# Decoder trunk in fp32: order of the products in the seven-product quads, one more such quad per layer, another split of the buffers

## The chip, the cores and the metric

One NeuronCore of a Trainium2 chip runs the whole program; the other cores have no work. The metric is the device time of one execution in microseconds. Engines named below: TensorE (PE in the profile, matmul and transpose), VectorE (DVE), ScalarE (ACT), GpSimd (POOL; here it mostly issues transfers) and SyncE (SP; its queue issues the weight loads).

## The reference

Two post-norm layers over 256 tokens of width 2048. Each layer mixes tokens with two attention groups (a sparse one with a top-k indexer, and a latent one, whose low-rank latents `cq` and `ckv` go through an RMS norm) and then runs a SwiGLU feed-forward of width 5632.

```python
proj = einsum('bsd,de->bse', x, w_in)
out_a = sparse_attention(...)                      # qa, ka, va, indexer qi, ki, wi
q_b  = rms_norm(cq, g_cq) @ w_uq;  kv = rms_norm(ckv, g_ckv) @ w_ukv
x = layer_norm(ALPHA * x + concat(out_a, out_b) @ w_o)
h = silu(x @ w_gate) * (x @ w_up)                  # w_gate, w_up: 2048 x 5632
x = layer_norm(ALPHA * x + h @ w_down)
```

## The kernel before

**Tiles and splits.** Tokens stand in two tiles of 128. Weights arrive in units of 128 x 1024 fp32 (two contraction slices of 128 x 512 columns, 512 KB). A unit is loaded by SP into a `raw` buffer; ScalarE rounds it into `wh` (line 324) and VectorE makes the rest `wl = raw - wh` (line 325). A `wh` and a `wl` are a pair. A product of two slices is six matmuls of 512 columns: `wh` with the high and with the low part of the tokens, `wl` with the high part, for each slice (lines 346 to 348, and 932 to 935 in the feed-forward).

**The feed-forward.** The 5632 columns go in 11 blocks of 512. Block 0 is done plainly (`gu`, 8 units for gate, 8 for up). Blocks 1 to 10 run `gate_up`: four quads, each over a unit `u`, its partner `u + 4`, gate and up. A plain quad (N) multiplies 2 tokens tiles x 2 units x 2 matrices, 8 products. A seven-product quad (S, `wino_quad`) is the Strassen-Winograd form: 7 products, from four matrix blocks `r11`, `r21` (gate), `r22` (up) and `r12`, the last the sum of two up units that a second, accumulating transfer on GpSimd's queue makes in a `sum` buffer; three more sums are made by VectorE in place in the raw buffers. Its token operands `s1` to `s4` are made once per layer (`sum_operands`). Block 1 was N N N S, block 2 is N S N S, blocks 3 to 10 are S S N S. In the last quad of a block VectorE also combines the product banks into gate and up: the lines with `on(...)`, line 970 in the profile, tiles `e` and `g`. Banks 2 and 3 hold `p6` and `p7`; `c11`, `c21` lie in banks 4 and 5, `c12` and `c22` in the pair named `att`.

**The order.** From block 3 on, `down_half` runs ahead of each `gate_up`: two columns of the down projection of earlier blocks, 8 units, 96 matmuls; its first column uses banks 2 and 3. A scheduler that works from priorities lays each engine's instructions into one fixed order when the kernel is built; at run time each engine follows its order and waits where an operand or a buffer is not ready. Work beside the matmuls (`spawn`, `tick`) is spread in steps: `yield n` lets `n` units of matmul work pass. `hidden` (lines 898 to 903) ends a block: silu, a product `g = g * e`, a transpose. `affine` (lines 431 to 434) is a layer norm's gain and bias, in blocks 0 to 2, from broadcast loads `g` and `b`.

**Buffers in the phase called more** (the last pass of the output projection, the feed-forward, and the first input block of the next layer): raw buffers 4 and 1 more, pairs 5 and 3 more, two sum buffers. A raw buffer is taken again after as many loads as there are buffers. The first pass of such a phase multiplies all 8 units of a matrix with the first token tile while the second tile is still being normalised, then the same 8 units with the second.

**The latents.** `tb_post` (line 587) normalises both latents and transposes them: for each of the two token tiles, transposes on TensorE into the two `tr` banks, then copies and differences by ScalarE and VectorE (`ckvT`, `cqT`, `kpT`).

Of the kernel before, what the change touches and what calls it, by code (L numbers as in the profile page):

```python
# [53 lines left out]
NKT = D // P  # L54
NFC = FFN // C
RAW = 4
UNITS, MORE = 5, 3
RAWMORE, RAWSUM = 1, 2
HALF = NKT // KU // 2
SOONER = 60  # L60
SOON = 200
# [19 lines left out]
def hybrid_trunk(ctx: ExitStack, tc: tile.TileContext, x, xt_in, pos, w_in, g_cq, g_ckv, w_uq,  # L81
                 w_ukv, w_o, ln1_g, ln1_b, ln1_T, w_gu, w_down, ln2_g, ln2_b, ln2_T, out):
    nc = tc.nc
# [6 lines left out]
    def nm(s):  # L90
        uid[0] += 1
        return f"{s}{uid[0]}"
# [23 lines left out]
    def t2(shape, s, dt=F32):  # L116
        if phase["name"] == "att":
            phase["t2"] = phase.get("t2", 0) + 1
            if phase["t2"] * T2MORE % (T2 + T2MORE) < T2MORE:
                return pt(shape, dt, s, "t2", T2MORE)  # L120
        return sb.tile(shape, dt, name=nm(s), tag="t2", bufs=T2)
# [17 lines left out]
    def trp():  # L139
        return in_turn("tr", 4, 2)  # L140
# [125 lines left out]
    def step(task):  # L266
        try:
            task[0] = units_gone[0] + (next(task[1]) or 1)
        except StopIteration:
            tasks.remove(task)  # L270

    def tick():
        units_gone[0] += 1
        for task in list(tasks):
            if task in tasks and task[0] <= units_gone[0]:
                step(task)
# [242 lines left out]
    def layer(l, xh, xl, norms, last):  # L519
# [76 lines left out]
        def tb_post(o):  # L596
            gq = t2([P, QL], "gq")
            gk = t2([P, KVL], "gk")
            nc.gpsimd.dma_start(gq, g_cq[l].partition_broadcast(P))
            nc.gpsimd.dma_start(gk, g_ckv[l].partition_broadcast(P))  # L600
            ckv = t2([P, NT, KVL], "ckv")
            sd = []
            for t in range(NT):
                nc.scalar.activation(cq[t][:, 432:512], o[t][:, 0:80], AF.Copy)
                nc.scalar.activation(ckv[:, t, :], o[t][:, 80:336], AF.Copy)
                sd.append(dup_rope(o[t][:, 336:400], cosM[:, t], sinM[:, t], M_ROPE))
            ys = [(rms(ckv[:, t, :], KVL, gk), rms(cq[t], QL, gq)) for t in range(NT)]
            yield 3
            for t, (yk, yq) in enumerate(ys):
                yield 1  # L610
                tp, tq = trp(), trp()
                rms_T(yk, KVL, tp[:, P:])
                dup_T(sd[t], tp)
                rms_T(yq, QL, tq)
                rms_out(KVL, ckvT, t, tp[:, P:])
                dup_out(kpT, t, tp)
                rms_out(QL, cqT, t, tq)
# [136 lines left out]
        if l == 0:  # L754
            turn("att")
            o = in_chunk(QI0, load_xT)
# [3 lines left out]
        else:  # L760
            o = in_chunk(QI0, None, lambda: finish(*norms))
# [10 lines left out]
        o = in_chunk(TA)  # L772
        p_ta = spawn(ta_post(o))
        o = in_chunk(QI1)
        p_qi1 = spawn(heads_T(o, 8, I_DIM, I_ROT, cosI, sinI, qiT[1]))
        p_ix = spawn(indexer())
        o = in_chunk(TB)
# [5 lines left out]
        o = proj([(w_uq[2][l, u], range(u * KU, (u + 1) * KU)) for u in range(QL // P // KU)], cqk, C)  # L783
# [26 lines left out]
        for c in range(D // C):  # L810
            o = proj([(w_o[l, c, k // KU], range(k, k + KU)) for k in first], olhs, C)
# [79 lines left out]
        def slhs(name):  # L891
            return lambda k: sums[name, k]
# [23 lines left out]
        def gate_up(fc, order, between):  # L916


            o, begun = {}, set()

            def passes(name, lhs, ks, w, final):
                if name not in o:
                    if name in BANKS:
                        o[name] = bank(BANKS[name], "gu_" + name)
                    else:
                        pair = o["up"] = att()
                        o["c12"], o["c22"] = pair[:, 0, :], pair[:, 1, :]
                for j, k in enumerate(ks):
                    h, l = lhs(k)
                    a, b = w[0][:, j, :], w[1][:, j, :]  # L930
                    end = final and j == len(ks) - 1
                    mm(o[name], h, a, start=name not in begun, stop=False)  # L932
                    begun.add(name)
                    mm(o[name], h, b, start=False, stop=False)  # L934
                    mm(o[name], l, a, start=False, stop=end)  # L935

            def token(t):
                return lambda k: xk(t, k)

            def unit(u):  # L940
                return range(u * KU, (u + 1) * KU)

            def plain_quad(u, first, lastz):
                for i, col in enumerate(("c11 c21", "c12 c22")):
                    vs = (u, u + HALF)
                    ws = [load_unit(w_gu[i][l, fc, v], KU * C) for v in vs] if first else [None, None]
                    for a in range(2):
                        for b in range(2):


                            t, j = (a, b) if first else (b, a)
                            if ws[j] is None:
                                ws[j] = load_unit(w_gu[i][l, fc, vs[j]], KU * C)
                            name = col.split()[t]
                            passes(name, token(t), unit(vs[j]), ws[j], lastz and i == 1 and a == b == 1)
                        tick()

            def wino_quad(u, final):
                ADD, SUB = ALU.add, ALU.subtract
                r12 = load_sum(w_gu[1][l, fc, u], w_gu[1][l, fc, u + HALF])  # L960
                r11, r21, r22 = (load_raw(w_gu[i][l, fc, v], KU * C) for i, v in ((0, u), (0, u + HALF), (1, u + HALF)))

                def p(i, lhs, raw, ks):
                    w = parts(raw, KU * C)
                    name = INTO.get(i, i)
                    passes(name, lhs, ks, w, final)

                def on(d, x, y, op):
                    with tc.high_priority(offset=SOONER):
                        nc.vector.tensor_tensor(d, x, y, op=op)  # L970

                if final:
                    e = phase["pool"].tile([P, NT, C], F32, name=nm("e"), tag="e", bufs=1)
                    g = phase["pool"].tile([P, NT, C], F32, name=nm("g"), tag="silu", bufs=1)
                lo_, hi_ = unit(u), unit(u + HALF)
                p("p1", token(0), r11, lo_)
                if final:
                    with tc.high_priority(offset=SOONER):
                        nc.scalar.activation(e[:, 0, :], o["p1"], AF.Copy)
                p("p2", token(0), r21, hi_)  # L980
                if final:
                    on(g[:, 0, :], e[:, 0, :], o["c11"], ADD)
                tick()
                nc.vector.tensor_tensor(r11, r12, r11, op=ADD)
                p("p6", slhs("s2"), r11, lo_)
                if final:
                    on(e[:, 0, :], o["p6"], e[:, 0, :], SUB)
                nc.vector.tensor_tensor(r21, r11, r21, op=ADD)
                p("p7", slhs("s3"), r12, lo_)
                if final:  # L990
                    on(e[:, 1, :], e[:, 0, :], o["p7"], ADD)
                tick()
                p("p4", token(1), r21, hi_)
                if final:
                    on(g[:, 1, :], o["c21"], e[:, 1, :], SUB)
                nc.vector.tensor_tensor(r11, r11, r22, op=SUB)
                p("p5", slhs("s1"), r11, lo_)
                if final:
                    on(e, e, o["p5"].unsqueeze(1).to_broadcast([P, NT, C]), ADD)
                tick()  # L1000
                p("p3", slhs("s4"), r22, lo_)
                if final:
                    on(e, e, o["up"], ADD)
                tick()
                if final:
                    return g, e

            lastp = max(i for i, q in enumerate(order) if q[0] == "plain")
            for i, (kind, u) in enumerate(order):
                if kind == "plain":  # L1010
                    plain_quad(u, i == 0, i == lastp)
                else:
                    r = wino_quad(u, i == len(order) - 1)
                if i == 0 and between:
                    between()
            return r
# [40 lines left out]
        def finish_hidden():  # L1057
            finish(*[h[2] for h in held])

        ORDER = {1: "NNNS", 2: "NSNS"}  # L1060
        UNIT = {"NNNS": (0, 1, 2, 3), "NSNS": (0, 2, 1, 3), "SSNS": (1, 2, 0, 3)}

        g = gu(0, 0, lambda: finish(*norms))
        affine(ln1_g[l], ln1_b[l], 0, ALPHA)
# [4 lines left out]
        for fc in range(1, NFC):  # L1069
            order = ORDER.get(fc, "SSNS")  # L1070
            if fc >= FIRSTD:
                down_half(fc)
                finish_hidden()
            g, u = gate_up(fc, [({"N": "plain", "S": "wino"}[k], v) for k, v in zip(order, UNIT[order])],
                           finish_hidden if fc < FIRSTD else None)
# [72 lines left out]
```

## Time and profile before

| what | value |
|---|---|
| three runs | 2189.41, 2189.73 and 2197.02 us, median 2189.73 |
| the profiled execution | 2196.58 us, of which the span from first to last instruction is 2194.5 us |
| mean granted TensorE clock | 0.997 |
| TensorE, matmul | busy 2157.3 us |
| VectorE | busy 1741.2 us |
| ScalarE | busy 1238.0 us |
| transfers | 204 GB/s read and written over the span |

The busy time of an engine is the union of its instructions' durations; matmuls overlap, so the start-to-start distance, not the printed duration, is what one costs. The profiled execution is one of the slower kind: it stands 6.9 us above the median of the runs.

### The profile page before, as it was taken

What the parts mean: (1) busy time and instruction counts of PE and PEld (TensorE: products, weight loads), DVE (VectorE), ACT (ScalarE), POOL (GpSimd) and SP (SyncE); (2) the same over time, 40 slices, a digit from 0 to 9 for tenths busy, and PEclk for the clock granted to TensorE, in tenths of its full rate; (3) what the DMA queues carried; (4) which work ended last, traced back from release to release, by engine and by line L of the source; (5) the groups of instructions that cost most, each with busy time, mean ns of one, the idle gap of its engine ahead of it and who ended that gap; (6) DMA issues with size and microseconds to landing.
All of it is one profiled execution on the core that took longest, in us unless ns stands there. A gap on an engine that the chain in (4) does not pass through costs nothing.

```text
span 2194.5 us, 28019 instructions
## 1 busy us (share of the span) xinstructions
PE 2157.3 (98%) x10044; PEld 1790.1 (82%) x10044; DVE 1741.2 (79%) x2227; ACT 1238.0 (56%) x1619; POOL 156.0 (7%) x254
## 2 busy tenths in 40 slices
PE   8999999999999999999999999999999999999997
PEld 7888888888888878888888888888887888877886
DVE  6685557889898889888657757678897889989885
ACT  5555454656565666656545554446565566656653
POOL 0100000001001011000101000000010001101101
PEclk9999999999999999999999999999999999999999
DMA  8544457557887787787745455666677788788785
GB/s 299 166 164 150 154 180 251 190 175 242 242 259 222 235 257 238 237 247 233 232 140 169 158 171 181 205 226 205 197 226 226 234 253 245 224 252 231 236 288 145
DMA packets 136364, 471.14 MB, mean 215 GB/s; under 512 B 15409, under 2 KB 15713, under 8 KB 135585
## 3 DMA queue, kind: packets, MB, share of 16 engines
q1 hardware_dynamic: 113760, 409.13, 54.8%
q0 software_dynamic: 22320, 60.09, 14.2%
q8 instruction: 79, 1.29, 0.2%
q14 instruction: 61, 0.49, 0.1%
q10 hardware_dynamic: 144, 0.13, 0.0%
HBM read 445.69 MB, written 2.10 MB: 204 GB/s over the span
## 4 chain that ended last, share of the span: by engine, by line
PE 66%; DVE 12%; issue 9%; DMA 9%; ACT 2%; POOL 1%; POOLq 0%; ACTq 0%; DVEq 0%; SPq 0%
PE acc L346 14%; PE acc L348 14%; PE acc L347 14%; DVE wl L325 7%; DMA raw<-in_w_gate_dram 4%; DMA raw<-in_w_down_dram 3%; PE tr L366 2%; ACT wh L324 2%; PE gu_p L932 2%; PE gu_p L935 2%; PE gu_p L934 2%; PE gu_c L932 2%; PE gu_c L935 2%; PE gu_c L934 2%; PE att L932 1%
## 5 line engine op out<-in xcount | busy, mean ns | idle before, releaser
L324 ACT ACTIVATE wh<-raw 128x1024 fp32r<-128x1024 f32 (+1 forms) x864 | 896.4, 1054 | 750.8 <-PE acc L348 208.1
L325 DVE TENSOR_TENSOR wl<-raw,wh 128x1024 fp32r<-128x1024 f32 (+1 forms) x864 | 1035.0, 1218 | 352.4 <-ACT wh L324 347.8
L346 PE MATMUL acc<-wh,xh 128*128 128x512 f32 (+1 forms) x768 | 304.1, 396 | 6.0 <-ACT wh L324 6.0
L348 PE MATMUL acc<-wh,xl 128*128 128x512 f32 (+1 forms) x768 | 298.6, 389 | 0.0
L347 PE MATMUL acc<-wl,xh 128*128 128x512 f32 (+1 forms) x768 | 297.6, 388 | 0.0
L346 PE MATMUL acc<-wh,hT 128*128 128x512 f32 x640 | 251.4, 393 | 13.7 <-DVE e L970 13.5
L347 PE MATMUL acc<-wl,hT 128*128 128x512 f32 x640 | 249.9, 390 | 0.0
L348 PE MATMUL acc<-wh,hT 128*128 128x512 f32 x640 | 249.8, 390 | 0.0
L346 PEld LDWEIGHTS acc<-wh,xh 128*128 128x128 f32 x768 | 145.2, 189 | 36.5 <-ACT wh L324 6.0
L348 PEld LDWEIGHTS acc<-wh,xl 128*128 128x128 f32 x768 | 144.9, 189 | 28.9 <-DVE xl L412 0.8
L347 PEld LDWEIGHTS acc<-wl,xh 128*128 128x128 f32 x768 | 145.3, 189 | 26.6 <-DVE wl L325 0.7
L932 PE MATMUL gu_c<-wh,xh 128*128 128x512 f32 x424 | 165.1, 389 | 0.0
L935 PE MATMUL gu_c<-wh,xl 128*128 128x512 f32 x424 | 165.0, 389 | 0.0
L934 PE MATMUL gu_c<-wl,xh 128*128 128x512 f32 x424 | 164.9, 389 | 0.0
L346 PEld LDWEIGHTS acc<-wh,hT 128*128 128x128 f32 x640 | 120.5, 188 | 44.0 <-DVE e L970 18.5
L348 PEld LDWEIGHTS acc<-wh,hT 128*128 128x128 f32 x640 | 120.6, 188 | 25.3
L347 PEld LDWEIGHTS acc<-wl,hT 128*128 128x128 f32 x640 | 120.5, 188 | 24.6
L313 POOL DMA_DIRECT2D sum<-in_w_up_dram x54 | 46.2, 856 | 906.5 <-DVE wl L325 396.3
L1035 POOL DMA_DIRECT2D x<-d x80 | 74.3, 1070 | 495.5 <-ACT d L1034 490.9
L935 PEld LDWEIGHTS gu_c<-wh,xl 128*128 128x128 f32 x424 | 79.6, 188 | 16.7
L934 PEld LDWEIGHTS gu_c<-wl,xh 128*128 128x128 f32 x424 | 79.6, 188 | 16.6
L932 PEld LDWEIGHTS gu_c<-wh,xh 128*128 128x128 f32 x424 | 79.6, 188 | 16.5
(287 smaller groups left out, 3552.8 us busy)
## 6 DMA issues: line engine op xcount, KB each, us to landing
raw<-in_w_gate_dram SPq DMA_DIRECT2D x176, 512.0 KB, 5.2
raw<-in_w_down_dram SPq DMA_DIRECT2D x176, 512.0 KB, 6.1
raw<-in_w_in_dram SPq DMA_DIRECT2D x144, 512.0 KB, 3.6
raw<-in_w_up_dram SPq DMA_DIRECT2D x122, 512.0 KB, 4.6
raw<-in_w_o_dram SPq DMA_DIRECT2D x64, 512.0 KB, 4.3
sum<-in_w_up_dram SPq DMA_DIRECT2D x54, 512.0 KB, 3.3
sum<-in_w_up_dram POOLq DMA_DIRECT2D x54, 512.0 KB, 8.4
x<-d POOLq DMA_DIRECT2D x80, 256.0 KB, 7.9
```

What stands on the lines that cost most here:

```text
L313: nc.gpsimd.dma_start(raw, b, accum_op=ALU.add)
L324: nc.scalar.activation(wh[:, :n], raw[:, :n], AF.Copy)
L325: nc.vector.tensor_tensor(wl[:, :n], raw[:, :n], f(wh[:, :n]), op=ALU.subtract)
L346: mm(o[t][:, :n], h, a, start=first, stop=False)
L347: mm(o[t][:, :n], h, b, start=False, stop=False)
L348: mm(o[t][:, :n], l, a, start=False, stop=final)
L366: nc.tensor.transpose(psum[:, i * P:(i + 1) * P], s, ident)
L932: mm(o[name], h, a, start=name not in begun, stop=False)
L934: mm(o[name], h, b, start=False, stop=False)
L935: mm(o[name], l, a, start=False, stop=end)
L1035: nc.gpsimd.dma_start(xt[t][:, c * C:(c + 1) * C], d, accum_op=ALU.add)
```

## The change

Five things, in the diff below. (1) In a seven-product quad the product `p3` is made third, ahead of the sums, and the last sum is written over the block `r22` that `p3` has read instead of over `r11`; the bank pair of up is added into `e` ahead of `p5`. The order of the products is now p1 p2 p3 p6 p7 p4 p5; it was p1 p2 p6 p7 p4 p5 p3. (2) Pairs in the phase called more go from eight to seven. (3) Raw buffers go from five to seven. (4) Block 1 becomes N S N S, so each layer has one seven-product quad more. (5) The latents of the first token tile are transposed one unit of matmul work earlier; those of the second stay where they were.

```diff
--- before.py
+++ after.py
@@ -54,8 +54,8 @@
 NKT = D // P
 NFC = FFN // C
 RAW = 4
-UNITS, MORE = 5, 3
-RAWMORE, RAWSUM = 1, 2
+UNITS, MORE = 5, 2
+RAWMORE, RAWSUM = 3, 2
 HALF = NKT // KU // 2
 SOONER = 60
 SOON = 200
@@ -607,7 +607,8 @@
             ys = [(rms(ckv[:, t, :], KVL, gk), rms(cq[t], QL, gq)) for t in range(NT)]
             yield 3
             for t, (yk, yq) in enumerate(ys):
-                yield 1
+                if t:
+                    yield 2
                 tp, tq = trp(), trp()
                 rms_T(yk, KVL, tp[:, P:])
                 dup_T(sd[t], tp)
@@ -981,26 +982,25 @@
                 if final:
                     on(g[:, 0, :], e[:, 0, :], o["c11"], ADD)
                 tick()
+                p("p3", slhs("s4"), r22, lo_)
                 nc.vector.tensor_tensor(r11, r12, r11, op=ADD)
                 p("p6", slhs("s2"), r11, lo_)
                 if final:
                     on(e[:, 0, :], o["p6"], e[:, 0, :], SUB)
+                tick()
                 nc.vector.tensor_tensor(r21, r11, r21, op=ADD)
                 p("p7", slhs("s3"), r12, lo_)
                 if final:
                     on(e[:, 1, :], e[:, 0, :], o["p7"], ADD)
-                tick()
+                nc.vector.tensor_tensor(r22, r11, r22, op=SUB)
                 p("p4", token(1), r21, hi_)
                 if final:
                     on(g[:, 1, :], o["c21"], e[:, 1, :], SUB)
-                nc.vector.tensor_tensor(r11, r11, r22, op=SUB)
-                p("p5", slhs("s1"), r11, lo_)
+                    on(e, e, o["up"], ADD)
+                tick()
+                p("p5", slhs("s1"), r22, lo_)
                 if final:
                     on(e, e, o["p5"].unsqueeze(1).to_broadcast([P, NT, C]), ADD)
-                tick()
-                p("p3", slhs("s4"), r22, lo_)
-                if final:
-                    on(e, e, o["up"], ADD)
                 tick()
                 if final:
                     return g, e
@@ -1057,8 +1057,8 @@
         def finish_hidden():
             finish(*[h[2] for h in held])
 
-        ORDER = {1: "NNNS", 2: "NSNS"}
-        UNIT = {"NNNS": (0, 1, 2, 3), "NSNS": (0, 2, 1, 3), "SSNS": (1, 2, 0, 3)}
+        ORDER = {1: "NSNS", 2: "NSNS"}
+        UNIT = {"NSNS": (0, 2, 1, 3), "SSNS": (1, 2, 0, 3)}
 
         g = gu(0, 0, lambda: finish(*norms))
         affine(ln1_g[l], ln1_b[l], 0, ALPHA)
```

What moves, engine by engine. First SP's loads around the last quad of a block (block 4 of layer 0; the `in_w_gate` and `in_w_up` loads at the top are that quad's own, the `in_w_down` loads belong to the down half that follows it). Before:

```order
L306 DMA raw_5666<-in_w_gate_dram 128x1024
L306 DMA raw_5668<-in_w_gate_dram 128x1024
L306 DMA raw_5670<-in_w_up_dram 128x1024
L306 DMA raw_5760<-in_w_down_dram 128x1024
L306 DMA raw_5778<-in_w_down_dram 128x1024
L312 DMA sum_6021<-in_w_up_dram 128x1024
L306 DMA raw_5796<-in_w_down_dram 128x1024
L306 DMA raw_5814<-in_w_down_dram 128x1024
L306 DMA raw_5840<-in_w_down_dram 128x1024
```

Now:

```order
L306 DMA raw_5676<-in_w_gate_dram 128x1024
L306 DMA raw_5678<-in_w_gate_dram 128x1024
L306 DMA raw_5680<-in_w_up_dram 128x1024
L306 DMA raw_5770<-in_w_down_dram 128x1024
L306 DMA raw_5788<-in_w_down_dram 128x1024
L306 DMA raw_5806<-in_w_down_dram 128x1024
L306 DMA raw_5824<-in_w_down_dram 128x1024
L306 DMA raw_5850<-in_w_down_dram 128x1024
L312 DMA sum_6031<-in_w_up_dram 128x1024
L306 DMA raw_5868<-in_w_down_dram 128x1024
```

The sum for a later quad stood ahead of the third down load and now stands ahead of the sixth. What the order does not show: the third down load takes the buffer of the last quad's `r11` before, of a plain unit loaded ahead of that quad now.

Next ScalarE around the latents in layer 0 (`rel` are the indexer's scores; `tr_1131` and `tr_1132` before, `tr_1113` and `tr_1114` now, are the first token tile's two banks, `tr_1176` the second's). Before:

```order
L636 ACTIVATE rel_1105<-att_1100 128x512
L636 ACTIVATE rel_1107<-att_1100 128x512
L324 ACTIVATE wh_1272<-raw_1270 128x1024
L369 ACTIVATE ckvT_396<-tr_1131 128x2x128
L369 ACTIVATE cqT_395<-tr_1132 128x4x128
L563 ACTIVATE kpT_390<-tr_1131 128x128
L324 ACTIVATE wh_1293<-raw_1291 128x1024
L636 ACTIVATE rel_1168<-att_1163 128x512
```

Now:

```order
L637 ACTIVATE rel_1105<-att_1100 128x512
L369 ACTIVATE ckvT_396<-tr_1113 128x2x128
L637 ACTIVATE rel_1107<-att_1100 128x512
L369 ACTIVATE cqT_395<-tr_1114 128x4x128
L563 ACTIVATE kpT_390<-tr_1113 128x128
L324 ACTIVATE wh_1272<-raw_1270 128x1024
L324 ACTIVATE wh_1293<-raw_1291 128x1024
L637 ACTIVATE rel_1168<-att_1163 128x512
```

The three readings of the first tile's banks moved ahead of two weight roundings and into the scores; the second tile's reading keeps its row. VectorE's difference for `ckvT` stood behind seven small rows of the top-k and a weight difference, and now stands among the scores.

Last, VectorE in block 1 of layer 0, from the end of the gain and bias on (`x_64`, `x_65` are the token tiles; `hT` belongs to block 0). Before:

```order
L325 TENSOR_TENSOR wl_4222<-raw_4219,wh_4221 128x1024
L370 TENSOR_TENSOR hT_4034<-tr_4103,hT_4034 128x4x128
L370 TENSOR_TENSOR hT_4034<-tr_4110,hT_4034 128x4x128
L433 TENSOR_TENSOR x_64<-x_64,g_4368 128x512
L433 TENSOR_TENSOR x_65<-x_65,g_4368 128x512
L325 TENSOR_TENSOR wl_4240<-raw_4237,wh_4239 128x1024
L325 TENSOR_TENSOR wl_4258<-raw_4255,wh_4257 128x1024
L434 TENSOR_TENSOR x_64<-x_64,b_4369 128x512
L434 TENSOR_TENSOR x_65<-x_65,b_4369 128x512
L325 TENSOR_TENSOR wl_4285<-raw_4276,wh_4284 128x1024
```

Now:

```order
L325 TENSOR_TENSOR wl_4171<-raw_4132,wh_4170 128x1024
L991 TENSOR_TENSOR raw_4134<-raw_4132,raw_4134 128x1024
L325 TENSOR_TENSOR wl_4183<-sum_4129,wh_4182 128x1024
L370 TENSOR_TENSOR hT_4034<-tr_4103,hT_4034 128x4x128
L370 TENSOR_TENSOR hT_4034<-tr_4110,hT_4034 128x4x128
L995 TENSOR_TENSOR raw_4136<-raw_4132,raw_4136 128x1024
L325 TENSOR_TENSOR wl_4195<-raw_4134,wh_4194 128x1024
L433 TENSOR_TENSOR x_64<-x_64,g_4378 128x512
L325 TENSOR_TENSOR wl_4205<-raw_4136,wh_4204 128x1024
L325 TENSOR_TENSOR wl_4218<-raw_4215,wh_4217 128x1024
L325 TENSOR_TENSOR wl_4236<-raw_4233,wh_4235 128x1024
L325 TENSOR_TENSOR wl_4254<-raw_4251,wh_4253 128x1024
```

Where plain units followed, the seven-product quad's parts and sums now stand. From the end of the last row on `b_4025`, just ahead of these, up to and with the row `g = g * e` that ends block 1, VectorE had 37 rows, 23 of 1024 columns and 14 of 512; it has 44 now, 30 and 14. The transposes that read this `g` stand 36 matmuls into block 2, before and now. Layer 1 has the same rows.

One more place, in words: in the first pass the eighth unit's pair can only be made when the first unit's pair is done with, so TensorE's order now has the first unit's six matmuls with the second token tile ahead of the eighth unit. From the end of those six to the first use of the eighth `wh` stand five matmuls and a transpose group, to the first use of its `wl` four matmuls more.

## Rows read from the trace of the kernel before

**Rows 1.** The page, part 1: busy time, share of span, instructions

```profile
PE 2157.3 (98%) x10044; PEld 1790.1 (82%) x10044; DVE 1741.2 (79%) x2227; ACT 1238.0 (56%) x1619; POOL 156.0 (7%) x254
```

**Rows 2.** TensorE's waits: who ended them, total us, times, longest

```profile
PE acc L346 <- DVE e L970: 13.5, 9, 4.3
...
PE tr L366 <- ACT kpT L563: 3.5, 2, 1.9
PE att L932 <- DVE e L970: 1.3, 1, 1.3
```

**Rows 3.** Timeline, TensorE, 1667 to 1675 us: start, duration, idle before

```profile
1667.39 0.39 PE L935 MATMUL att<-wh,many 128*128 128x512 f32 x1
...
1669.43 0.39 PE L348 MATMUL acc<-wh,hT 128*128 128x512 f32 x1
1674.12 0.65 PE L346 MATMUL acc<-wh,hT 128*128 128x512 f32 x1 [4.30 <-DVE e L970]
```

**Rows 4.** Timeline, 1661 to 1674 us: VectorE, ScalarE, DMA issues, landing

```profile
1666.81 0.69 DVE L970 TENSOR_TENSOR e<-gu_p,e 128x512 f32<-128x512 f32 x1
1672.24 1.22 DVE L325 TENSOR_TENSOR wl<-raw,wh 128x1024 fp32r<-128x1024 f32 x1 [4.75 <-ACT wh L324]
1673.39 0.68 DVE L970 TENSOR_TENSOR e<-e,gu_p 128x512 f32<-128x512 f32 x1
...
1671.16 1.06 ACT L324 ACTIVATE wh<-raw 128x1024 fp32r<-128x1024 f32 x1 [6.20 <-DMA raw<-in_w_down_dram]
...
1661.62 12.20 SPq L306 DMA_DIRECT2D raw<-in_w_down_dram  x6
...
raw<-in_w_down_dram SPq DMA_DIRECT2D x176, 512.0 KB, 6.1
```

**Rows 5.** Windows: length, busy time of each engine, granted clock, DMA

```profile
117.20:121.20 4.00, 3.29 (x12) 2.91 (x13) 3.31 (x8) 3.23 (x7) 0.00 (x0) 0.58 0.43 140
1674.10:1678.00 3.90, 3.88 (x10) 3.06 (x11) 3.90 (x5) 3.89 (x5) 0.00 (x0) 0.56 0.77 234
776.00:780.00 4.00, 3.07 (x13) 2.55 (x14) 3.69 (x5) 2.59 (x3) 0.00 (x0) 1.00 1.03 406
```

**Rows 6.** Timeline, 102 to 118 us: TensorE, ScalarE, VectorE

```profile
107.36 1.13 PE L631 MATMUL att<-kiT,qiT 64*128 64x256 f32 x8
...
111.28 0.38 PE L366 MATMUL tr<-ident,rn 128*128 128x128 f32 x2
...
117.91 0.69 PE L366 MATMUL tr<-ident,rn 128*128 128x128 f32 x2 [1.88 <-ACT kpT L563]
...
117.58 0.28 ACT L563 ACTIVATE kpT<-tr 128x128 f32<-128x128 f32 x1 [4.28 <-DVE ckvT L370]
...
102.95 0.75 DVE L585 SCALAR_TENSOR_TENSOR rn<-cq,rrs,gq 128x512 f32<-128x512 f32 x1 [0.34 <-POOL rrs L584]
...
117.13 0.42 DVE L370 TENSOR_TENSOR ckvT<-tr,ckvT 128x256 fp32r<-128x256 f32 x1
```

**Rows 7.** Windows over feed-forward blocks 3 to 10, layer 0: their sum

```profile
sum 504.40, PE 499.48 PEld 412.16 DVE 448.40 ACT 306.49 POOL 46.30; mean PE 62.43 PEld 51.52 DVE 56.05 ACT 38.31 POOL 5.79
```

**Rows 8.** Timeline, blocks 1 and 2 of layer 0: VectorE, then TensorE

```profile
443.81 1.29 DVE L433 TENSOR_TENSOR x<-x,g 128x512 f32<-128x512 f32 x2 [1.90 <-ACT g L431]
445.48 1.29 DVE L434 TENSOR_TENSOR x<-x,b 128x512 f32<-128x512 f32 x2 [0.37 <-ACT b L431]
...
466.88 4.63 DVE L325 TENSOR_TENSOR wl<-raw,wh 128x1024 fp32r<-128x1024 f32 x4
...
486.15 1.22 DVE L903 TENSOR_TENSOR g<-g,e 128x1024 f32<-128x1024 f32 x1
...
488.07 1.03 PE L366 MATMUL tr<-ident,g 128*128 128x128 f32 x8
```

**Rows 9.** A weight pair's ScalarE copy; ScalarE at the first pass

```profile
L324 ACT ACTIVATE wh<-raw 128x1024 fp32r<-128x1024 f32 (+1 forms) x864 | 896.4, 1054 | 750.8 <-PE acc L348 208.1
...
401.01 1.50 ACT L409 ACTIVATE v<-att,gbT 128x128 f32<-128x128 f32 x4 [0.33 <-ACT v L409]
```

## The prediction

> **What bounds the kernel now.** The page first: TensorE is busy for 98% of the span [rows 1], so time is won by fewer matmuls or fewer waits of TensorE. The timeline [rows 3] gives the price of a matmul of 512 columns: 9 starts in 2.04 us, 0.227 us each. It also shows that a wait costs 0.16 us more than the idle time printed, since 4.69 us lie between the two starts where 0.227 would, 4.46 too many, and 4.30 are printed. The waits by releaser come next [rows 2]: 13.5 us in nine waits of the down projection's first matmul on VectorE's `e` rows, 3.5 us in two waits of the latents' transposes on ScalarE's `kpT`, 1.3 us at the start of block 2's `att`. The timeline behind the longest tells the mechanism [rows 4]. VectorE finished `e` from p6 at 1667.5 and came to `e` from p7, which empties the bank that down wants, only at 1673.4. It stood 4.75 us before a `wl` row, for a `wh` that ScalarE could not make until a down load landed. Issue of the six down loads behind the sum began at 1661.6, when the last quad gave buffers back, and a down load takes 6.1 us to land in the median. So the cause is five raw buffers, three of them held by the last quad. VectorE is not short of time: in blocks 3 to 10 it is busy 56.05 us against 62.43 us of TensorE [rows 7]. Last the clock [rows 5]: behind this wait it was granted 0.56 for 3.9 us, behind the first latent wait 0.58 for 4.0 us (the lower level, 1.2 instead of 2.4 GHz, for most of that time), so each cost 0.44 x 3.9 or 0.42 x 4.0, 1.7 us more.
>
> **(a) Fewer matmuls.** A seven-product quad has one product of two slices, 6 matmuls, less. Two layers: 12 x 0.227 = **-2.7 us**.
>
> **(b) Latents.** The second tile's transposes at 117.91 waited for the first tile's `kpT`, which waited 4.28 us for VectorE's `ckvT` difference at 117.13, although the first tile had been transposed at 111.28 [rows 6]. Now these transposes stand right behind the score matmuls that begin at 107.36, 12 matmuls (2.7 us) earlier, and the copies and differences move ahead of weight work and top-k rows. Their data is there: the first tile's last latent row on VectorE began at 102.95 and took 0.75. The wait was shorter than the move, and VectorE's rows in front of the difference go too, so I take both waits and the one clock loss as gone: 3.5 + 2 x 0.16 + 1.7 = **-5.5 us**; the other bound is 0.
>
> **(c) Raw buffers, seven for five.** Three down parts still stand ahead of `e` from p7, but the first four down loads now take the buffers of plain units, free long before, and the sum no longer stands in front of the third. The fifth takes that of `r11`, released when the last sum is written; VectorE then has seven rows of 1024 columns and four of 512 to do before that load's part, 10 us by the prices under (d), against 6.1. So the nine waits should go: 13.5 + 9 x 0.16 + 1.7 for the clock = 16.6 us. I take nine tenths, **-15 us**, since loads that land late can leave some; the bounds are 0 and -16.6. Seven pairs instead of eight cost nothing there: VectorE's 6.4 us of slack per block hide the shorter lead. Without that cover it is up to one product, 1.36 us, for each of the 16 blocks.
>
> Against this stands a rule. The Trainium skill (Trainium Kernel Development and Optimization, Key Constraints) says that transfers of all queues run on the same 16 DMA engines and interleave. By it more loads in flight would only land later each, and (c) would be 0. The trace is in between: 0.77 and 1.03 of the DMA engines were busy in two short stretches [rows 5].
>
> **(d) Block 1 with two such quads.** A plain quad turned into a seven-product one needs 3 more parts and 3 more sums on VectorE, and the last rows of the quad stand closer; the order has 7 rows more up to the product `g = g * e`. A row of 1024 columns costs (4.63 - 1.22) / 3 = 1.14 us, one of 512 columns 1.29 - 0.69 = 0.60 [rows 8]. The gain and bias rows that wait for their broadcast loads end at 445.48 + 1.29 = 446.8. Between there and the end of `g = g * e` VectorE now has 30 x 1.14 + 14 x 0.60 = 42.5 us of rows, so it ends at 489.3 at the earliest; it had 34.5 us of rows and ended at 487.4 with 6.1 us of waiting. TensorE would come to the transposes of this `g` at 488.07 - 1.36 - 1.46 (the wait at `att`, which the earlier addition of the up banks takes away) = 485.25. It waits 4.0 us, there or spread over the first half of block 2 (`c21`, too, needs its bank emptied by such a row). The nearest bounds: if the broadcast loads come early enough to spare VectorE the 1.90 and 0.37 us in front of those rows, 1.7 us; if it waits as long as before, 10.1. I take 5 for each layer, near the lower end since more loads are under way early: **+10 us**, and **-1.5** for the wait at `att`. Behind this, block 2 holds no new gain rows, and VectorE regains its lead in the plain quad.
>
> **(e) The first pass with seven pairs.** The eighth unit is now rounded after the first unit's second-tile matmuls, in the open. ScalarE's copy is 1.05 us, VectorE's difference 1.22 [rows 4, 9], against 9 matmuls, 2.04 us, that TensorE does meanwhile: 0.2 us if both start at once, up to 1.5 more behind a group of norm rows on ScalarE [rows 9]. Three such passes; the two that precede block 1 vanish in (d), where VectorE is late anyway. **+0.7 us**, bounds 0 and 2.
>
> **The sum.** -2.7 - 5.5 - 15 + 10 - 1.5 + 0.7 = -14.0. The profiled execution took 2196.6 us (span 2194.5, 2.1 around it): 2182.6. The runs mostly took 2189.5, 7 less; I suppose that this long wait [rows 3] with its clock loss, 6 us, is what these do not have, so that (c) is worth 6 less there: 2189.7 - 8.0 = 2181.7. I forecast **2182 us**, with 2174 to 2189 as this case's own range.
>
> **The rivals.**
>
> *VectorE keeps up in blocks 1 and 2.* For it: before, it waited 6.1 us in that stretch, so its rows end when operands come, and an early start of loads helps; (d) at 2 x 1.7, all of (c) less 6: 2189.7 - 2.7 - 5.5 - 10.6 + 3.4 - 1.5 + 0.7 = 2173.5. Against it: 42.5 us of rows in line.
>
> *The waits before down stay*, because the loads land later when more are under way. For it: the busy DMA engines [rows 5]; against it: the down loads are asked for a whole quad earlier. With a third of (c), 3 us in the runs' terms: 2189.7 - 2.7 - 5.5 - 3 + 10 - 1.5 + 0.7 = 2187.7, up to 2191 with none.
>
> *The clock falls in block 2.* The new waits there are of 1 to 4 us, two in a layer. The clock fell behind a wait of 1.88 us and behind one of 4.30, but in the window from 776 on, which holds another of the nine, it stayed at 1.00 [rows 5]. If it falls at all four, 4 x 1.7 = 6.8 more: 2189. The Trainium skill (TensorE: Matmul & The Clock Gate, What's actually happening) has the clock at half after an idle stretch until the engine has been busy again; the two windows agree, the third does not settle when.
>
> *Slower: the banks of down.* p7 was followed by three products before down wants its bank, 4.08 us; now by two, 2.72. If VectorE still comes to `e` from p7 late, because three down parts and now a shorter lead in pairs stand ahead, every one of the 16 down halves waits 1.36 us longer and (c) gains nothing: 2189.7 - 2.7 - 5.5 + 10 - 1.5 + 0.7 + 21.8 = 2212.5. It decides as soon as VectorE is 2.7 us behind TensorE at the end of a block; the 6.4 us of slack speak against.
>
> **Chances.** Forecast 0.52, VectorE keeps up 0.17, waits stay 0.15, clock 0.08, banks 0.08. The range from 2170 to 2194 takes in all but the last case and the edges. A change of 0.5%, 10.9 us, is about what a measurement tells from none: faster is below 2178.8. Of the forecast's own range some 0.37 lies there (0.19), with all of the second case: 0.36. Slower, above 2200.7: 0.08. Within 0.5%: 0.56.
>
> **What would show it.** (a) 12 matmuls fewer. (b) No wait on `kpT`, granted clock near 1 at 118 us. (c) The nine waits on `e` before `acc` gone, VectorE's waits for `wh` shorter, and down loads that land before the quad ends. (d) Waits at `gu_c` or at the transposes of `g` in block 2 of both layers, some 5 us each, with VectorE busy throughout. (e) Short waits at the eighth unit. The prediction is wrong if (d) shows no wait, or if the waits of (c) are still there.

## The result, and the profile after

The changed kernel takes **2169.04 us** (median of 6 runs, 2168.84 to 2170.31). The kernel before, run beside it, takes 2192.80 us (6 runs, 2187.06 to 2200.20). The ratio is 0.9891, with a 95% interval from 0.9870 to 0.9913: 1.1% faster. The prediction was 2182 with a range from 2170 to 2194, so the time lies 1 us below the range; the gain was 23.8 us where 8 were forecast.

The page of the changed kernel, its span and the first engines (busy time, share of the span, instructions), and the first line of the chain of work that ended last; the same line of the kernel before stands below it:

```profile
span 2167.0 us, 28036 instructions
PE 2146.7 (99%) x10032; PEld 1785.2 (82%) x10032; DVE 1748.9 (81%) x2239; ACT 1251.5 (58%) x1625; POOL 157.4 (7%) x256
PE 92%; DVE 3%; issue 2%; DMA 2%; ACT 1%; POOL 0%; POOLq 0%; DVEq 0%; SPq 0%; ACTq 0%
```

```profile
PE 66%; DVE 12%; issue 9%; DMA 9%; ACT 2%; POOL 1%; POOLq 0%; ACTq 0%; DVEq 0%; SPq 0%
```

TensorE has 12 matmuls fewer than in [rows 1] and is busy for 99%. The spans differ by 27.5 us. All waits of TensorE after the change (what waited on what: total us, times, longest):

```profile
PE acc L346 <- ACT wh L324: 6.3, 1, 6.3
PE tr L366 <- DVE g L904: 2.1, 2, 1.1
PE gu_c L933 <- DVE g L971: 0.3, 1, 0.3
PE tr L366 <- DVE lg L485: 0.2, 1, 0.2
```

Of [rows 2] nothing is left: no wait on `e`, none on `kpT`, none at `att`. The 6.3 us are the first load of the program, 6.0 before. New are two waits of the transposes of `g`, one in block 2 of each layer.

The same place as [rows 4], the last quad of a block and the start of down, in the timeline after (start, duration; first SP's issues, then VectorE, then TensorE's first matmul of down):

```profile
1630.81 13.43 SPq L306 DMA_DIRECT2D raw<-in_w_down_dram  x5
1646.15 3.98 SPq L306 DMA_DIRECT2D raw<-in_w_down_dram  x3
...
1650.82 0.68 DVE L971 TENSOR_TENSOR e<-gu_p,e 128x512 f32<-128x512 f32 x1
1651.42 1.22 DVE L325 TENSOR_TENSOR wl<-raw,wh 128x1024 fp32r<-128x1024 f32 x1
1652.56 0.68 DVE L971 TENSOR_TENSOR e<-e,gu_p 128x512 f32<-128x512 f32 x1
...
1654.48 0.39 PE L346 MATMUL acc<-wh,hT 128*128 128x512 f32 x1
```

A down half has eight such loads. Four of them now go out in a row from 1630.81 on and a fifth at 1643.91; before, only two went out early and the other six began at 1661.62 [rows 4]. What counts is the load of the third down part, the last part ahead of p7's row. It is now issued at 1633.08, 21.4 us ahead of the first down matmul (1654.48). Before, it was issued at 1662.92, 6.7 us ahead of the time at which that matmul was due, 1674.12 - 4.46 = 1669.66 [rows 3]; it took 8.1 us to land, and ScalarE's copy that waited for it began at 1671.16 [rows 4]. The issue after, then the two early ones, the issue and its landing before:

```profile
1633.08 0.33 SPq L306 DMA_DIRECT2D raw<-in_w_down_dram  x1
```

```profile
1646.28 8.56 SPq L306 DMA_DIRECT2D raw<-in_w_down_dram  x2
...
1662.92 0.33 SPq L306 DMA_DIRECT2D raw<-in_w_down_dram  x1
...
raw<-in_w_down_dram SPq DMA_DIRECT2D x1, 512.0 KB, 8.1
```

In the kernel after, VectorE does its `wl` row without a wait where it stood 4.75 us, empties p7's bank at 1653.24, and TensorE starts down 0.23 us behind its last matmul (1654.25), at the ordinary distance.

Blocks 1 and 2 of layer 0, where the forecast put 10 us of new waits for both layers (GpSimd's load of the gain, VectorE's gain and bias rows, the product `g = g * e`, TensorE's transposes):

```profile
431.41 0.54 POOL L422 DMA_DIRECT2D g<-in_ln_g_dram  x1 [29.83 <-DVE few L370]
...
435.61 1.30 DVE L433 TENSOR_TENSOR x<-x,g 128x512 f32<-128x512 f32 x2
437.32 1.29 DVE L434 TENSOR_TENSOR x<-x,b 128x512 f32<-128x512 f32 x2 [0.41 <-ACT b L431]
...
481.56 1.22 DVE L904 TENSOR_TENSOR g<-g,e 128x1024 f32<-128x1024 f32 x1
...
482.83 1.09 PE L366 MATMUL tr<-ident,g 128*128 128x128 f32 x8 [1.05 <-DVE g L904]
```

The gain and bias rows end at 437.32 + 1.29 = 438.6, which is 7.25 us behind the first matmul of block 1 (431.36). Before it was 446.8 [rows 8] against 435.26, 11.5 us.

### The profile page after: what moved, and what is told of

Same layout as the page of the kernel before. It is cut to its first block, busy times and chain, and to the rows that moved or that the text cites. A ratio compares the mean times of both kernels' runs of the same rounds, so it can differ in the third digit from the quotient of the medians.

```text
span 2167.0 us, 28036 instructions
## 1 busy us (share of the span) xinstructions
PE 2146.7 (99%) x10032; PEld 1785.2 (82%) x10032; DVE 1748.9 (81%) x2239; ACT 1251.5 (58%) x1625; POOL 157.4 (7%) x256
## 3 DMA queue, kind: packets, MB, share of 16 engines
q0 software_dynamic: 22608, 61.14, 14.6%
q8 instruction: 79, 1.29, 0.2%
## 4 chain that ended last, share of the span: by engine, by line
PE 92%; DVE 3%; issue 2%; DMA 2%; ACT 1%; POOL 0%; POOLq 0%; DVEq 0%; SPq 0%; ACTq 0%
PE acc L346 17%; PE acc L347 17%; PE acc L348 16%; PE gu_p L935 4%; PE gu_p L936 4%; PE gu_p L933 4%; PE gu_c L935 4%; PE gu_c L936 4%; PE gu_c L933 4%; PE att L935 3%; PE att L936 3%; PE att L933 3%; PE tr L366 2%; DVE wl L325 1%; PE acc L838 1%
## 5 line engine op out<-in xcount | busy, mean ns | idle before, releaser
L347 PEld LDWEIGHTS acc<-wl,xh 128*128 128x128 f32 x768 | 144.8, 188 | 27.5 <-DVE wl L325 1.8
L933 PE MATMUL gu_p<-wh,many 128*128 128x512 f32 x240 | 93.4, 389 | 0.0
L935 PE MATMUL gu_p<-wl,many 128*128 128x512 f32 x240 | 93.4, 389 | 0.0
L936 PE MATMUL gu_p<-wh,many 128*128 128x512 f32 x240 | 93.4, 389 | 0.0
```

The costliest lines, as they stand in the source:

```text
L347: mm(o[t][:, :n], h, b, start=False, stop=False)
```

## The experiments

Each kernel ran beside the kernel before on the same chip; kernels of one group below share those runs. The changed kernel measured 2169.04 us at first and 2168.75 us beside the third group; where a kernel is compared with it across groups, the comparison rests on that agreement. The **theory** after the first reading: the gain is the raw buffers (down loads no longer wait for a buffer) and the latents, and the second quad in block 1 was cheap because the gain rows come early. The **rivals**: the new order of the products gave it; both are needed; either is enough.

**First group: buffers against order.** The kernel before took 2190.72 us here (19 runs, 2186.84 to 2201.43).

*Only the buffers, in the kernel before.*

```diff
-UNITS, MORE = 5, 3
-RAWMORE, RAWSUM = 1, 2
+UNITS, MORE = 5, 2
+RAWMORE, RAWSUM = 3, 2
```

> The kernel before with only the buffers of the change: seven raw buffers instead of five, seven pairs instead of eight. Theory 'raw buffers': the down loads come early enough, the nine waits of the down projection's first matmul on e go, and with them 13 to 18 us: 2175 to 2180 us. Rival 'product order' (p3 moved up and the sum over its block is what lets VectorE come to e from p7 in time): the waits stay, 2188 to 2193 us. Rival 'both are needed': also 2188 or more. If seven pairs are too few, some other wait grows, up to 1.36 us for each of 16 blocks.

Measured 2172.87 us (4 runs, 2171.88 to 2174.07), ratio 0.9911 [0.9883, 0.9938]. TensorE's waits:

```profile
PE acc L346 <- ACT wh L324: 6.3, 1, 6.3
PE tr L366 <- ACT kpT L563: 3.5, 2, 1.9
PE acc L348 <- DVE xl L412: 0.5, 1, 0.5
```

The waits on `e` are gone, the latents' waits are untouched, and 17.8 us are won, 2 us beyond the theory's band and more than the 15 of the forecast. Seven raw buffers and seven pairs suffice.

*Only the order of products and sums, in the kernel before* (the two hunks on the quad of the change and nothing else).

> The kernel before with only the products of the seven-product quad in the changed order and the last sum over r22; buffers, block 1 and latents as before. Theory 'raw buffers': the nine waits on e stay, only the 1.3 us at att go: 2188 to 2193 us. Rival 'product order': the nine waits go: 2175 to 2180 us. Rival 'banks' (two products behind p7 instead of three): the waits get longer, above 2196 us.

Measured 2197.16 us (10 runs, 2195.61 to 2200.62), ratio 1.0027 [1.0011, 1.0043]: slower. TensorE's waits, without the latents' two and a small one:

```profile
PE acc L346 <- DVE e L970: 9.5, 17, 2.6
PE acc L346 <- ACT wh L324: 9.4, 5, 6.0
PE tr L366 <- DVE g L903: 3.3, 2, 2.2
PE acc L347 <- DVE wl L325: 0.8, 1, 0.8
```

There are 17 waits on `e` instead of nine [rows 2], in the down halves of both layers. The time is 4 us above the band that the theory named and inside that of the rival of the banks. The rival's picture fits only in part: the waits on `e` are more, but shorter, 9.5 us against 13.5 with a longest of 2.6 against 4.3. The loss comes from waits elsewhere, 3.3 us on `g` in block 2 of both layers and 3.4 us more on `wh`. All waits, with 0.16 us for each, are 31.2 us against 28.2; the spans differ by 3.8. With eight pairs VectorE's order now has four down parts ahead of the row that empties p7's bank; the kernel before has three, the changed kernel three, the kernel of `b_raw7` two. Here are VectorE's rows, as built, from the first down part to the row of p7, first of the kernel before, then with the new order alone (the last row of each reads p7's bank, every `wl` row is a down part):

```text
L325 TENSOR_TENSOR wl_8323<-raw_8320,wh_8322 128x1024
L970 TENSOR_TENSOR g_8233<-e_8232,gu_c_8004 128x512
L325 TENSOR_TENSOR wl_8341<-raw_8338,wh_8340 128x1024
L970 TENSOR_TENSOR e_8232<-gu_p_8016,e_8232 128x512
L325 TENSOR_TENSOR wl_8359<-raw_8356,wh_8358 128x1024
L970 TENSOR_TENSOR e_8232<-e_8232,gu_p_8028 128x512
```

```text
L325 TENSOR_TENSOR wl_8323<-raw_8320,wh_8322 128x1024
L970 TENSOR_TENSOR g_8233<-e_8232,gu_c_8004 128x512
L325 TENSOR_TENSOR wl_8341<-raw_8338,wh_8340 128x1024
L325 TENSOR_TENSOR wl_8359<-raw_8356,wh_8358 128x1024
L970 TENSOR_TENSOR e_8232<-gu_p_8027,e_8232 128x512
L325 TENSOR_TENSOR wl_8377<-raw_8374,wh_8376 128x1024
L970 TENSOR_TENSOR e_8232<-e_8232,gu_p_8039 128x512
```

*The changed kernel with five raw buffers.*

```diff
-RAWMORE, RAWSUM = 3, 2
+RAWMORE, RAWSUM = 1, 2
```

> The kernel after with five raw buffers instead of seven, the seven pairs kept. Theory 'raw buffers': the waits on e are back in the down projection, 13 to 20 us: 2182 to 2190 us. Rival 'product order' or 'either is enough': 2169 to 2173 us. For block 1 of two such quads: if the early gain and bias rows come from the raw buffers, their last row ends 10 us or more behind the block's first matmul and the waits in block 2 are 3 to 5 us a layer; if not, they stay at 1.7.

Measured 2185.89 us (10 runs, 2182.94 to 2188.05), ratio 0.9968 [0.9953, 0.9983]: 17 us slower than the changed kernel, as the theory had it, but not in the place it named. TensorE's waits:

```profile
PE gu_c L933 <- DVE g L971: 4.8, 2, 2.4
PE acc L346 <- DVE e L971: 2.2, 5, 0.8
PE tr L366 <- DVE g L904: 1.7, 1, 1.7
PE att L933 <- ACT wh L324: 0.8, 1, 0.8
```

Only 2.2 us stand before down; 8.2 us (4.8, 1.7 and 0.8 above, and two waits on `wl`, 0.9 together) stand in block 2 of the two layers. The gain rows nevertheless begin as early as with seven buffers:

```profile
436.19 1.29 DVE L433 TENSOR_TENSOR x<-x,g 128x512 f32<-128x512 f32 x2
437.99 1.29 DVE L434 TENSOR_TENSOR x<-x,b 128x512 f32<-128x512 f32 x2 [0.50 <-ACT b L431]
```

They end at 439.3, 7.7 us behind the block's first matmul (431.57). So the early start is not the raw buffers' doing. What they save in block 2 is VectorE's waits for `wh` between 440 and 495 us: 4.0 us with five, 1.2 with seven. Neither branch of the expectation for block 1 came true: the rows are early and the waits are 4 us a layer all the same. All printed waits are 8.2 us more than in the changed kernel (17.1 against 8.9, nine more of them), and one stretch of the lower clock behind the wait of 2.4 us costs 1.7 us more (its window stands further down); of the 15.5 us between the spans some 4 are not assigned.

*The changed kernel with the old order of products and sums.* (The quad as in the kernel before.)

> The kernel after with the products and sums of the seven-product quad in the old order (p3 last, last sum over r11, up added last). Theory 'raw buffers': 2169 to 2173 us, at most the waits at att (0.3 to 1.3 us) are back. Rival 'product order' or 'both are needed': waits on e in front of down, 2180 us or more.

Measured 2168.13 us (4 runs, 2167.38 to 2169.44), ratio 0.9889 [0.9862, 0.9917], 0.9 us below the theory's band. The order gives nothing with these buffers. The two waits on `g` of the changed kernel are gone as well, and a short one at `att` stands in their place:

```profile
PE att L933 <- DVE e L971: 0.6, 1, 0.6
```

**Second group: latents, block 1, pairs, and the size of the raw pool.** The kernel before: 2191.33 us (21 runs, 2182.54 to 2200.50).

*The changed kernel with the latents as before.*

```diff
-                if t:
-                    yield 2
+                yield 1
```

> The kernel after with the latents of the first tile transposed one unit later again, as before. Theory 'the two waits on kpT are on the path': both are back (3.5 us, 0.3 us around them, and 1.7 us of clock at the first one): 2174.5 us, 5.5 more than after. Rival 'hidden or paid elsewhere' (what TensorE gains there it loses at the next wait): 2169 to 2171 us.

Measured 2173.03 us (6 runs, 2171.99 to 2175.09), ratio 0.9926 [0.9903, 0.9948]: 4.0 us more than the changed kernel's median, between the waits alone (3.5 + 0.3) and the waits with the clock (5.5). Both waits on `kpT` are back, 3.5 us as in [rows 2]. The profiled execution lost the clock behind the first; the kernel with only the buffers had the same wait of 1.9 us there and did not (window, busy time of PE, PEld, DVE, ACT, POOL, granted clock, DMA share, GB/s; `a_lat0`, then `b_raw7`):

```profile
117.20:121.20 4.00, 3.24 (x11) 2.88 (x12) 3.31 (x8) 3.23 (x7) 0.00 (x0) 0.59 0.45 139
```

```profile
117.20:121.20 4.00, 3.07 (x17) 2.68 (x18) 3.31 (x7) 3.12 (x7) 0.00 (x0) 1.00 0.39 131
```

Six kernels have this wait of 1.9 us. In that window three show a lower clock (0.58 before, 0.59 in `a_lat0`, 0.73 in `b_order`) and three 1.00 (`b_raw7`, `b_raw6`, `b_pairs7`).

*The changed kernel with block 1 as before.*

```diff
-        ORDER = {1: "NSNS", 2: "NSNS"}
+        ORDER = {1: "NNNS", 2: "NSNS"}
```

> The kernel after with block 1 of three plain quads and one seven-product quad again. It does 12 matmuls more (2.7 us) and loses the waits of block 2 in both layers. Theory 'the second such quad in block 1 cost 3.4 us, since the gain and bias rows begin early': 2167.5 to 2169.5 us, with those waits gone and the first gain rows later against the block's first matmul. Rival 'it cost the 8.5 us that were forecast, and something else gave more': 2162 to 2165 us. Rival 'it cost nothing': 2171 to 2172 us.

Measured 2169.30 us (6 runs, 2168.20 to 2169.94), ratio 0.9907 [0.9885, 0.9929]. The waits of block 2 are gone, the 12 matmuls are back, and the time is that of the changed kernel within 0.3 us, as the theory had it. The second such quad costs about what its matmuls save.

*The kernel before with seven pairs and five raw buffers.*

```diff
-UNITS, MORE = 5, 3
+UNITS, MORE = 5, 2
```

> The kernel before with seven pairs instead of eight, five raw buffers kept. Theory 'pairs cost nothing there': 2187 to 2193 us, as before. Rival 'the pairs are part of it' (a shorter lead of VectorE lengthens the waits, so that raw buffers alone would give more than they did): 2195 us or more.

Measured 2187.48 us (10 runs, 2182.46 to 2191.42), ratio 0.9979 [0.9959, 0.9999]. The time fits the theory, but the waits do not:

```profile
PE acc L346 <- ACT wh L324: 7.6, 4, 5.9
PE att L934 <- DVE wl L325: 2.3, 3, 0.8
PE gu_p L932 <- ACT d L1034: 2.1, 3, 1.0
PE att L932 <- ACT wh L324: 1.4, 1, 1.4
PE acc L346 <- DVE e L970: 1.2, 2, 0.8
```

One pair fewer leaves two down parts ahead of p7's row instead of three, and the waits on `e` fall from 13.5 to 1.2 us. TensorE now waits for the operands themselves, since loads still lack buffers. The wait has moved.

*Six raw buffers and seven pairs, in the kernel before* (`MORE = 2`, `RAWMORE = 2`).

> The kernel before with six raw buffers and seven pairs. Theory 'the number of raw buffers sets how long a down load waits for its issue': between five and seven, 2176 to 2186 us, with some of the nine waits left. Rival 'a threshold': as with seven (2172 to 2174 us) if one more buffer is enough for the load that was late, or as with five (2188 or more) if not.

Measured 2175.71 us (8 runs, 2174.42 to 2177.88), ratio 0.9939 [0.9921, 0.9957]. One more buffer gives 11.8 of the 14.6 us between five (`b_pairs7`) and seven (`b_raw7`): nearer to the threshold than to an even share. It lies in neither band, 0.3 us below the theory's and 1.7 above the rival's, and no wait on `e` is left.

**Third group: whether the parts add up.** The kernel before: 2190.55 us (9 runs, 2184.45 to 2195.30).

*The changed kernel again, as the measure for this group.*

> The kernel after once more, so that the three beside it are compared with it on one chip. Both theories: 2168 to 2171 us.

Measured 2168.75 us (4 runs, 2167.89 to 2170.23), ratio 0.9904 [0.9887, 0.9920].

*The old order of the products again.*

> The kernel after with the old order of products and sums, once more beside after. Theory 'the order costs its waits in block 2 and gives nothing with seven raw buffers': 1 to 2.5 us faster than after. Rival 'no difference': within 0.5 us.

Measured 2167.97 us (4 runs, 2167.23 to 2168.75), ratio 0.9899 [0.9883, 0.9916]: 0.8 us faster than the changed kernel, between the two bands; in the first group it was 0.9. Each single ratio leaves room for no difference, but it is the fastest version of the study in both groups.

*The kernel before with buffers and latents only* (the edit of `b_raw7`, and the latents' hunk of the change).

> The kernel before with the buffers and the latents of the change, but the old order of products and one seven-product quad in block 1. Theory 'buffers and latents are the whole gain; the new order and the second quad cancel': within 1.5 us of after. Rival 'the other two parts give something as well': 3 us or more slower than after.

Measured 2169.08 us (5 runs, 2168.21 to 2171.73), ratio 0.9909 [0.9892, 0.9926]. Within 0.4 us of the changed kernel: three of the five parts (pairs, raw buffers, latents) are the whole gain. Beside the version above, which has the second quad as well (2167.97), the quad saves 1.1 us with the old order, less than the spread of the runs.

*The changed kernel with the buffers of before* (`MORE = 3`, `RAWMORE = 1`).

> The kernel after with the buffers of before, five raw and eight pairs. Theory 'the gain rows of block 0 begin late because of the eighth pair': the gain loads are issued 3 us or more behind the first matmul of block 1 again, the rows end 10 us or more behind it, and the waits in block 2 are 4 us or more a layer; with the waits in front of down the time is 2185 to 2197 us. Rival 'the order N S N S itself brings them early': gain rows end 8 us or less behind the first matmul, the waits in block 2 as with five raw and seven pairs (5 us a layer) or less.

Measured 2208.33 us (5 runs, 2202.56 to 2209.35), ratio 1.0078 [1.0060, 1.0095]: 39.6 us above the changed kernel, and slower than the kernel before by 17.8. TensorE's waits, then GpSimd's load and VectorE's gain rows:

```profile
PE acc L346 <- DVE e L971: 15.0, 20, 4.4
PE gu_c L933 <- DVE g L971: 12.5, 4, 5.7
```

```profile
435.04 0.54 POOL L422 DMA_DIRECT2D g<-in_ln_g_dram  x1 [31.89 <-DVE few L370]
439.76 1.29 DVE L433 TENSOR_TENSOR x<-x,g 128x512 f32<-128x512 f32 x2 [0.93 <-ACT g L431]
441.03 1.29 DVE L434 TENSOR_TENSOR x<-x,b 128x512 f32<-128x512 f32 x2
```

The load is issued 3.3 us behind the first matmul of block 1 (431.78) and the rows end 10.5 behind it; with seven pairs and the same five raw buffers it was 0.3 and 7.7. Block 2 now holds 6 us of waits a layer (12.5 / 2). The time is 11 us above the band of the expectation: the waits before down grew to 15.0 us in 20, from 13.5 in nine. The eighth pair is what makes the gain rows late. In the nine kernels with seven pairs the first of these loads is issued less than 0.7 us behind the first matmul of block 1, in the three with eight 3.3 to 3.7. The path to it is argued from VectorE's order and not shown by itself: with a weight row more done ahead, VectorE's other rows, `few` among them, on which the load waits, come later.

## Why the prediction was wrong

**(a) Fewer matmuls: right.** 10044 to 10032, 2.7 us.

**(b) Latents: right in mechanism, 1.5 us too large.** Both waits went. Undoing it costs 4.0 us, not 5.5; adding it to the buffers gives 3.8 (2172.87 to 2169.08, two groups). The clock loss was counted as certain, and three of the six traces with this wait show it. The Trainium skill (TensorE: Matmul & The Clock Gate, What's actually happening) says that the windows in which the chip judges the engine run free of the kernel; the two rows above fit this, since an equal wait cost the clock in one and not in the other, but no run here shows such windows.

**(c) Raw buffers: the mechanism was right, the size was not; this is the first of two steps that failed.** The trace's waits gave 16.6 us, I took 15 and then struck off 6, supposing that the runs at 2189.5 lacked the longest wait. No row showed that. The buffers alone give 17.8 us in medians of runs (13.6 to 25.6 by the interval), and the wait at `att` (1.5, put down to the early addition) goes with them too: `b_raw7` has none. So 9 + 1.5 were forecast, 7.3 too few. The nine waits on `e` by themselves are not the price of the lack: with seven pairs and five raw buffers they fall to 1.2 us and the time only by 3.9, since TensorE then waits for the operands (`b_pairs7`). With more runs the kernel before has medians of 2190.6 to 2192.8, not 2189.7, and runs from 2182.5 to 2200.5 in one group of 21; the profiled 2196.6 lies among them. With seven raw buffers the runs of a kernel spread by 1.5 to 3.5 us. What fits this, and was not shown by itself, is that the waits for a buffer vary with the moment at which loads land, so that the runs of the kernel before hold more or less of them, and none is without.

"Seven pairs cost nothing there" was wrong the other way: with five raw buffers the eighth pair cost, 3.9 us in the kernel before (`b_pairs7`, 0.2 to 9.0 by the interval) and 22.4 in the changed one (2208.33 against 2185.89, two groups). So 14.6 of the 17.8 us are the two raw buffers at seven pairs (`b_pairs7` to `b_raw7`, two groups), and 3.2 the pair; seven raw buffers with eight pairs were not run. The eighth pair put one more down part ahead of p7's row (three against two in the old order, four against three in the new one) and made the gain rows late.

The rule weighed there, that transfers of all queues share 16 engines and interleave (Trainium Kernel Development and Optimization, Key Constraints, in the Trainium skill), is borne out in part. The issues of the changed kernel, four down loads between 1630.5 and 1635 us, then the one between 1643 and 1644.5 (the last number is the median time to landing), and for comparison the six of the kernel before between 1660 and 1674:

```profile
raw<-in_w_down_dram SPq DMA_DIRECT2D x4, 512.0 KB, 9.5
```

```profile
raw<-in_w_down_dram SPq DMA_DIRECT2D x1, 512.0 KB, 3.2
```

```profile
raw<-in_w_down_dram SPq DMA_DIRECT2D x6, 512.0 KB, 8.0
```

Loads in flight together do land later each, in both kernels. In both stretches a sum transfer of GpSimd was in flight as well (here that of the changed kernel), and the runs do not part its share from theirs:

```profile
sum<-in_w_up_dram POOLq DMA_DIRECT2D x1, 512.0 KB, 10.2
```

Yet the gain was not zero: 9.5 us to land against a lead of 21.4 us for the third part's load, where it had been 8.1 against 6.7. The 6.1 us of the prediction, a median over the program, was too short for this place.

**(d) Block 1: the second step that failed is the start of VectorE's rows.** "The gain and bias rows end at 446.8" was carried over from the kernel before, although the change of pairs and order moves them. They end 7.25 us behind the block's first matmul, not 11.5, which is 4.3 us less. Seven pairs alone (`b_pairs7`) bring them to 8.8. With the 42.5 us of rows that I had counted, 438.6 + 42.5 + 1.2 us of waits for `wh` = 482.3, and `g = g * e` ends at 482.8: the rows were counted rightly. From the right start the lower end, 4.0 us a layer, would have been 0. The +10 measured 2.9 (2.4 printed in three waits, 0.16 more for each restart). The net of (a), (d) and the first part of (e), forecast at +7.3 or a little more, is -0.3 by `a_nnns`. The wait that is left, 1.05 us in layer 0, comes of the new order and the second quad together: with seven raw buffers and only one of the two (`a_nnns`, `a_oldord`) no wait on `g` stands there. The forecast's waits come true only with five raw buffers: 8.2 us printed in `a_raw5`, 12.5 in `a_buf58`.

**(e) The eighth unit: no wait.** Nothing stands there in the trace; the bound 0 was right.

**The rivals.** "VectorE keeps up", 2173.5, came nearest: it had (d) right and still struck 6 us off (c). "The waits before down stay" and "the clock falls in block 2" did not happen; the window behind the new wait has a clock of 1.00. The clock did fall there in `a_raw5`, behind a wait of 2.4 us (the second row):

```profile
482.00:486.00 4.00, 3.17 (x18) 2.79 (x19) 3.96 (x5) 2.47 (x4) 0.00 (x0) 1.00 0.00 0
```

```profile
479.00:482.00 3.00, 3.00 (x7) 2.42 (x8) 2.81 (x3) 2.55 (x4) 0.00 (x0) 0.50 0.92 365
```

"Slower: the banks of down" did not happen here. With the old buffers and the new order the waits before down do become more, 17 in `b_order` and 20 in `a_buf58` against nine, but with 9.5 and 15.0 us they stay short of the 21.8 that it was priced at, on top of the 13.5 of before.

**The sum.** Forecast was 2189.7 - 8.0, measured 2169.0, 12.7 us less. (c) with the wait at `att` makes 7.3 of that, (a) with (d) 7.6, (e) 0.7; (b) was 1.5 too large the other way, and the base 0.8 to 3.1 too low: together 11 to 13. In the trace, of the 27.5 us between the spans the waits on `e` are 16.6, the latents 5.5, the matmuls 2.7, `att` 1.5, two small waits 1.4; the new waits take 2.9 back and the start 0.3. About 3 us remain that I have not assigned to rows. The small waits, from the view of [rows 2]:

```profile
PE gu_p L932 <- ACT d L1034: 0.7, 1, 0.7
PE att L934 <- DVE wl L325: 0.4, 1, 0.4
```

## What to carry to other kernels

When a load waits for a buffer, count how far ahead of its use it is issued (6.7 us before, 21.4 after, for the load that the wait hung on) and set it against the time to land at that place, and take the waits that hang on it at full value; a wide spread of the runs went with the same lack here (5 to 18 us with five raw buffers, 1.5 to 3.5 with seven). A deeper pool of finished operands is no free lead: in an engine's fixed order it puts more rows ahead of the row that another engine waits for, and here a pair paid better as two raw buffers. When several edits move rows, read the start of a chain of rows anew in the changed order; a price worked out from the old start was 4.3 us off for each layer.

## What was not expected of the hardware

The same wait of 1.9 us of TensorE, at the same matmul, left the granted clock at 0.58 to 0.73 in three kernels and at 1.00 in three others. And loads that take three times as long to land (9.5 instead of 3.2 us, with four and a sum transfer in flight) cost nothing once they are issued early: the median landing of a down load rose from 6.1 to 6.3 us while the time fell by 1.1%.
